# Stick-breaking's queries and keys of a head pair in one 512-column product, with four PSUM banks for dense products and two for DeltaNet

## The chip, the cores and the metric

The kernel runs on one core of one Trainium2 chip. Its time is device microseconds (us) of one execution, and the median of several executions is what counts. The engines are TensorE (PE in the profile, with its weight loads as a row of their own, PEld), VectorE (DVE), ScalarE (ACT), GpSimd (POOL) and SyncE (SP), which issues most of the DMAs. PSUM, the memory that matmuls write, has eight banks, each 512 float32 columns wide over 128 partitions.

## What is computed

A decoder trunk of two layers on 512 tokens of width 1024. A layer is a SwiGLU FFN (half step), a mixer with two branches, and a second FFN.

```
def hybrid_mixer(h, w_in, ...):
    dn_qkv, dn_z, dn_b, dn_a, sb_q, sb_k, sb_v, gate_a, gate_b = split_cols(h @ w_in)
    ...                                             # conv + SiLU, L2 norm, decay
    o_a = gated_delta_rule_chunked(q, k, v, g, beta)            # branch A, 8 heads of 128
    y_a = (rmsnorm(o_a, dn_out_norm) * silu(dn_z)) @ w_branch_a
    qb = rmsnorm(to_heads(sb_q, 8, 128), sb_q_norm)             # branch B, 8 heads of 128
    kb = rmsnorm(to_heads(sb_k, 8, 128), sb_k_norm)
    o_b = stick_breaking_attention(qb, kb, to_heads(sb_v, 8, 128))
    y_b = o_b @ w_branch_b
    return (sigmoid(gate_a) * y_a + sigmoid(gate_b) * y_b) @ w_out

x = x + 0.5 * swiglu(rmsnorm(x), ffn1_w_in, ffn1_w_out)
x = x + hybrid_mixer(rmsnorm(x), ...)
x = x + 0.5 * swiglu(rmsnorm(x), ffn2_w_in, ffn2_w_out)
```

## The kernel before

**Dense products.** Every float32 operand is split into a high and a low part (`wh`, `wl` of a weight, `xh`, `xl` of the activation), and a product is three matmuls: high x high, low x high, high x low. ScalarE writes `wh`, VectorE `wl`, from a raw chunk of 1024 elements a partition (512 KB) that SP loads (`fetch`, L635). Two raw chunks and three converted ones are in flight. A "unit" of the mixer is one step of the string `ORDER` (L32), 70 letters that set the order of dense work within a mixer: D, G, Z and B units give 128 output columns over all tokens, feature-major (weights stationary, 512 tokens moving, 8 x 3 = 24 matmuls of 512 columns, one PSUM bank). D is a third of a DeltaNet head (q, k or v), G a branch gate, Z the DeltaNet output gate, B a piece of branch B's projection.

**Stick-breaking's units** (S, L1435) are token-major: tokens are stationary and 256 weight columns (two heads) move. Three S units in turn give a head pair's q, k and v. A unit has 2 chunks x 4 token blocks x 4 k-tiles x 3 = 96 matmuls of 256 columns, and fills two banks, each with two token blocks side by side (`proj_tm`, L772). Of q and k ScalarE evacuates a bank with four squares that sum as they go (`sbsq`, for the norms) and then one copy (`sraw`). After k the chain of that pair starts (`sb_chain`, `sb_head`).

**Work between dense matmuls.** The program is laid out ahead of time: `Weave` holds a model of every engine's time, and after each dense matmul (each third one in `proj_tm`) `tick` lets pending chains issue the steps that the model says are ready. TensorE's instructions run in that fixed order. Chains are the evacuations (`evac`, in order), weight conversions (`ahead`), the stick-breaking chain, and the DeltaNet chain of a head pair (`dn_chain`, L1167): norms (`pk`, `kw`), decays (`pd`), scores (`pq`, `lt`), an inverse by 31 steps on VectorE (`it`, `itmp`), two levels of blocks (`pp`, `pt_`), the recurrence over four token blocks (`pa`, then `rhs` and `qs`, then `py`, `po_`; `dn_recur`, L1355) and the output (`oT`, `oa`). A pair's scores wait until the pair before has done its levels (`dn_at`). `until` lets chains go on without dense work: a D unit that begins a pair waits so for the pair two before it, the letter C for the stick-breaking chains, and E drains everything left.

**PSUM.** Three pools (L362 to L364): `acc` with 3 banks for dense products, `dps` with 3 for DeltaNet, `sps` with 2 for the stick-breaking chain. `dps` also serves the FFN's second sum (`ps`), the transposes of x at the start (`xps`), and small sums. A chain asks for a tile with `room`, which waits in the model until the oldest tile of a full pool was last used; `bank` (L731) does the same for dense products by a count of evacuations that are pending.

Of the kernel before, what the change touches and what calls it, by code (L numbers as in the profile page):

```python
# [8 lines left out]
F32 = mybir.dt.float32  # L9
# [6 lines left out]
P = 128  # L16
# [12 lines left out]

ORDER = "DSDDDDGDSDSDDDDDSGSGSZSDSZSDDDSDGDSDDDGDDZDGZSGGZGZCGGGBBBBBBBBEZGGZGG"  # L32
SQ = 4
CB = 3


# [306 lines left out]
class Trunk:  # L343
    def __init__(self, ctx, tc, depth, w):
        self.tc = tc
        self.nc = self.weave = Weave(tc.nc)
        self.w = {n: [m[l] for l in range(depth)] for n, m in w.items()}
        self.ctx = ctx
        e = ctx.enter_context
        self.cst = e(self.pool("cst", 1))  # L350
        self.xop = e(self.pool("xop", 1))
        self.wp = e(self.pool("wp", 3))
        dram = e(tc.tile_pool(name="scr", bufs=1, space=bass.MemoryType.DRAM))
        self.scr_in = dram.tile([32, 32, 32], F32, name="scr_in")
        self.scr_out = dram.tile([32, 32, 32], F32, name="scr_out")
        self.osp = dram.tile([2, KD, P, SEQ], F32, name="osp")
        self.ysp = dram.tile([KD, P, SEQ], F32, name="ysp")
        self.gsp = dram.tile([NG, P, SEQ], F32, name="gsp")
        self.zsp = dram.tile([HEADS, P, SEQ], F32, name="zsp")
        self.xsp = dram.tile([KD, P, SEQ], F32, name="xsp")  # L360
        self.stat = e(self.pool("stat", 1))
        self.acc = e(self.pool("acc", 3, space=PSUM))  # L362
        self.dps = e(self.pool("dps", 3, space=PSUM))
        self.sps = e(self.pool("sps", 2, space=PSUM))  # L364
        self.order = list(self.weight_order(depth))
        self.chunks = iter([c for c in self.order if len(c) == 5])
        self.turn = iter(self.order)
        self.raws = []
        self.parts = []
        self.rings = ([], [])  # L370
        self.hid = None
        self.r = None
        self.evacs = [0, 0]
        self.convs = self.conv_done = 0
# [224 lines left out]
    def weight_order(self, depth):  # L599

        w = self.w

        def ffn(w_in, w_out):
            for kind, a, *b in PLAN:
                if kind == "c":
                    yield w_in, 0, KD, a % 2 * DFF + a // 2 * P, P
                elif kind == "s":
                    yield a, b[0]
                elif b[1] == 0:
                    yield (w_out,) + SECTIONS[a] + (b[0] * P, P)  # L610

        for l in range(depth):
            yield from ffn(w["ffn1_in"][l], w["ffn1_out"][l])
            yield w["in"][l], 0, KD, 4 * D, 16
            count = dict.fromkeys(ORDER, 0)
            for kind in ORDER:
                n = count[kind]
                count[kind] += 1
                if kind == "D":
                    yield w["in"][l], 0, KD, (1, 0, 2)[n % 3] * D + n // 3 * P, P  # L620
                elif kind == "S":
                    for k0 in (0, 4):
                        yield w["in"][l], k0, 4, N_SB + n % 3 * D + n // 3 * 2 * P, 2 * P
                elif kind == "G":
                    yield w["in"][l], 0, KD, N_GA + n * P, P
                elif kind == "Z":
                    yield w["in"][l], 0, KD, 3 * D + n * P, P
                elif kind == "B":
                    yield w["b"][l], 0, KD, n * P, P
            for m in ("a", "out"):  # L630
                for n in range(KD):
                    yield w[m][l], 0, KD, n * P, P
            yield from ffn(w["ffn2_in"][l], w["ffn2_out"][l])

    def fetch(self):  # L635
        c = next(self.chunks, None)
        if c is None:
            return
        src, k0, nk, c0, n = c
        raw = self.wp.tile([P, nk, n], F32, tag="raw", bufs=2, name="raw")  # L640
        self.nc.sync.dma_start(
            raw, src[k0 * P:(k0 + nk) * P, c0:c0 + n].rearrange("(k p) n -> p k n", p=P))
        self.raws.append(raw)

    def ahead(self):
# [84 lines left out]

    def bank(self, shape, n=1):  # L731

        self.weave.until(lambda: self.evacs[0] - self.evacs[1] <= 3 - n)
        return self.acc.tile(shape, F32, tag="acc", name="pf")

    def evac(self, engine, f):
# [35 lines left out]
    def proj_tm(self, ready=lambda: True):  # L772
# [20 lines left out]
            used[0] = True  # L793
        self.weave.until(ready)
        return out


    def fetch_fours(self):
# [633 lines left out]

    SBG = (((3, 0, 512),), ((2, 0, 384),), ((1, 0, 256), (0, 256, 128)))

    def sb_unit(self, l, n):  # L1435

        nc = self.nc
        m = self.sb
        pr, w = n // 3, n % 3
        if w == 0:  # L1440
            self.weave.until(lambda: self.weave.done(("sb", pr % 2)))
            self.sbq = dict(ss=m.tile([P, NTB, 4], F32, tag="sbss", bufs=2, name="sbss"))
        st = self.sbq
        if w < 2:
            pts = self.proj_tm()
            raw = st[w] = m.tile([P, NTB, 256], F32, tag=f"raw{w}", bufs=2, name="sraw")
            def half(a):
                sq = self.stat.tile([P, 2, 2, P], F32, tag="junk", name="sbsq")
                for b in range(2):
                    for hh in range(2):  # L1450
                        nc.scalar.activation(sq[:, b, hh, :], pts[a][:, b, hh * P:(hh + 1) * P], AF.Square,
                                             accum_out=st["ss"][:, 2 * a + b, 2 * w + hh:2 * w + hh + 1])
                nc.scalar.copy(raw[:, 2 * a:2 * a + 2, :], pts[a])

            self.evac("scalar", lambda: half(0))
            self.evac("scalar", lambda: half(1))
            if w == 1:
                chain = self.weave.after(("sb", pr % 2), self.sb_chain(l, pr, st))
                self.weave.spawn(self.weave.after("sb", self.weave.then("evac", chain)))
            return  # L1460
        pts = self.proj_tm(lambda: self.weave.done(("sb", (pr + 1) % 2)))
        vh = m.tile([P, NTB, 256], F32R, tag="vh", bufs=1, name="vh")
        vl = m.tile([P, NTB, 256], F32R, tag="vl", bufs=1, name="vl")
# [10 lines left out]
        self.evac("scalar", lambda: half(0))  # L1474
        self.evac("scalar", lambda: half(1))

    def sb_chain(self, l, pr, st):
        nc = self.nc
        m = self.sb
# [9 lines left out]
        for hh in range(2):  # L1489
            for w in range(2):  # L1490
                for b in range(NTB):
                    v = st[w][:, b, hh * P:(hh + 1) * P]
                    s = y[:, b, 2 * w + hh:2 * w + hh + 1]
                    nc.scalar.activation(v, v, AF.Copy, scale=s)
                yield 0
            yield from self.sb_head(l, pr * 2 + hh, hh, st)

    def sb_head(self, l, h, hh, st):
# [4 lines left out]
        for w in range(2):  # L1503
            yield from self.sps.room("sp")
            ps = self.sps.tile([P, SEQ], F32, tag="sp", name="qk_ps")
            for b in range(NTB):
                nc.tensor.transpose(ps[:, b * P:(b + 1) * P], st[w][:, b, cs], self.ident)
            hi = m.tile([P, SEQ], F32R, tag=f"qkh{w}", bufs=1, name="qkh")
            lo = m.tile([P, SEQ], F32R, tag=f"qkl{w}", bufs=1, name="qkl")
            g = (self.sbg if w == 0 else self.vcol["sbk"])[:, l:l + 1]  # L1510
# [159 lines left out]
    def mixer(self, l, gain_next):  # L1670
# [4 lines left out]
        with self.pool("mx", 1, reuse_waits="tile") as self.mx:  # L1675
# [12 lines left out]
            for kind in ORDER:  # L1688
# [3 lines left out]
                if kind == "D":  # L1692
                    self.dn_unit(l, n, first[1] if n == 0 else None)
                elif kind == "S":
                    self.sb_unit(l, n)
                elif kind in "GZ":
                    self.gate(kind, n)
                elif kind == "C":
# [138 lines left out]
```

## Time and profile before

| what | value |
|---|---|
| median of 3 runs (lowest to highest) | 2801.56 us (2798.18 to 2802.18) |
| the profiled execution: its time, its span | 2801.22 us, 2799.4 us |
| TensorE busy, instructions | 2755.9 us (98%), 17249 |
| weight loads, DVE, ACT, POOL busy | 2449.7, 2009.1, 1468.2, 232.9 us |
| mixer of layer 0 | about 378 to 1055 us from the span's start |
| mixer of layer 1 | about 1763 to 2440 us |
| DMA | 312.46 MB, 112 GB/s |

How to read a row: a group of instructions shows its engine, operation, what it writes and reads (`pf<-xh,wh`: into the dense tile pf, moving xh, stationary or second operand wh), the shape, the count, busy time and mean duration, and the idle time of the engine before it with what ended it. All kernel lines appear as L286, the helper that issues them, so groups are told apart by the names of their tiles. Busy times of matmuls overlap, since a matmul's end is modelled.

### The profile page before, as it was taken

The numbers are of one execution on the slowest core, as the hardware profiler recorded it, in microseconds if no ns is written. First come the engines' busy times: TensorE is split into PE (matmuls) and PEld (weight loads), VectorE is DVE, ScalarE is ACT, GpSimd is POOL, SyncE is SP. The second block draws the span as 40 slices with busy tenths as digits, with TensorE's granted clock in tenths as the row PEclk, the third lists the DMA queues.
The fourth block names the chain that finished last, engine by engine and source line by source line (L and its number), as shares of the span: only waits on it lengthen the run. The fifth ranks groups of instructions, "written<-read, shape, count | busy, mean of one in ns | idle before, by whom it ended". The sixth has DMA issues, their size and how long they took to land.

```text
span 2799.4 us, 44209 instructions
## 1 busy us (share of the span) xinstructions
PE 2755.9 (98%) x17249; PEld 2449.7 (88%) x17249; DVE 2009.1 (72%) x3154; ACT 1468.2 (52%) x2953; POOL 232.9 (8%) x243
## 2 busy tenths in 40 slices
PE   8999999999999999999999999999999999999999
PEld 7999988888888887999979999889988888879998
DVE  6877576886777557867678676778878765588664
ACT  4444346767664644544445344468675745445333
POOL 4000020000100031000010000110001001210000
PEclk9999999999999999999999999999999999999999
DMA  4333143323335654333143331423323358433332
GB/s 145 117 106 111 39 121 92 91 80 88 89 101 180 225 170 128 102 106 106 49 136 102 105 107 54 114 80 86 102 80 94 103 162 285 148 91 112 99 91 64
DMA packets 438017, 312.46 MB, mean 112 GB/s; under 512 B 31706, under 2 KB 408080, under 8 KB 437808
## 3 DMA queue, kind: packets, MB, share of 16 engines
q1 hardware_dynamic: 436432, 308.99, 37.1%
q8 instruction: 135, 2.21, 0.3%
q10 hardware_dynamic: 1088, 0.53, 0.1%
q14 instruction: 74, 0.61, 0.1%
q0 software_dynamic: 288, 0.12, 0.0%
HBM read 276.03 MB, written 33.55 MB: 111 GB/s over the span
## 4 chain that ended last, share of the span: by engine, by line
PE 86%; DVE 9%; ACT 3%; DMA 1%; issue 1%; ACTq 0%; DVEq 0%
PE pf L286 56%; PE pq L286 16%; PE ps L286 7%; DVE wl L286 1%; DVE itmp L286 1%; ACT u L286 1%; PE sbo_ps L286 1%; DVE sbs L286 1%; DVE qkv L286 1%; PE z_ps L286 1%; DVE it L286 1%; DMA raw<-in_ffn_w_out_dram 1%; PE pa L286 1%; PE at_ps L286 0%; DVE tl L286 0%
## 5 line engine op out<-in xcount | busy, mean ns | idle before, releaser
L286 ACT ACTIVATE wh<-raw 128x1024 fp32r<-128x1024 f32 (+2 forms) x352 | 337.1, 959 | 314.9 <-PE pf L286 147.4
L286 PE MATMUL pf<-xh,wh 128*128 128x512 f32 (+1 forms) x1312 | 487.8, 372 | 0.4 <-DVE t L286 0.4
L286 DVE TENSOR_TENSOR wl<-raw,wh 128x1024 fp32r<-128x1024 f32 (+2 forms) x351 | 402.4, 1147 | 117.7 <-ACT wh L286 115.0
L286 PE MATMUL pf<-xh,wl 128*128 128x512 f32 (+1 forms) x1312 | 485.5, 370 | 1.3 <-DVE wl L286 1.3
L286 PE MATMUL pf<-xl,wh 128*128 128x512 f32 (+1 forms) x1312 | 484.4, 369 | 0.0
L286 PE MATMUL pf<-hp,wh 128*128 128x512 f32 x1408 | 440.9, 394 | 4.6 <-ACT wh L286 4.6
L286 PEld LDWEIGHTS pf<-hp,wh 128*128 128x128 f32 x1408 | 265.8, 190 | 61.1 <-ACT wh L286 6.3
L286 DVE TENSOR_TENSOR wl<-sraw,wh 128x1024 fp32r<-128x1024 f32 x216 | 263.5, 1221 | 52.3 <-ACT wh L286 52.3
L286 ACT ACTIVATE wh<-sraw 128x1024 fp32r<-128x1024 f32 x216 | 228.2, 1056 | 137.8 <-PE pf L286 104.9
L286 PE MATMUL pf<-hp,wl 128*128 128x512 f32 x704 | 277.0, 393 | 9.1 <-DVE wl L286 9.1
L286 PEld LDWEIGHTS pf<-xh,wl 128*128 128x128 f32 x1312 | 247.7, 189 | 41.4 <-DVE wl L286 2.8
L286 PEld LDWEIGHTS pf<-xh,wh 128*128 128x128 f32 x1312 | 247.9, 189 | 39.5 <-issue 2.2
L286 PEld LDWEIGHTS pf<-xl,wh 128*128 128x128 f32 x1312 | 247.9, 189 | 38.9 <-issue 1.2
L286 PE MATMUL pq<-tl,wh 128*128 128x256 f32 x864 | 244.5, 283 | 0.0
L286 PE MATMUL pq<-th,wl 128*128 128x256 f32 x864 | 244.5, 283 | 0.0
L286 PE MATMUL pq<-th,wh 128*128 128x256 f32 x864 | 244.5, 283 | 0.0
L286 PE MATMUL pf<-wh,xh 128*128 128x256 f32 x768 | 226.7, 295 | 0.0
L286 PE MATMUL pf<-wl,xh 128*128 128x256 f32 x768 | 218.7, 285 | 0.0
L286 PE MATMUL pf<-wh,xl 128*128 128x256 f32 x768 | 218.3, 284 | 0.0
L286 DVE SCALAR_TENSOR_TENSOR x<-pf,x 128x512 f32<-128x512 f32 x128 | 87.8, 688 | 132.8 <-PE pf L286 132.6
L286 PEld LDWEIGHTS pf<-hp,wl 128*128 128x128 f32 x704 | 133.8, 190 | 39.0 <-DVE wl L286 11.0
L286 PEld LDWEIGHTS pq<-th,wh 128*128 128x128 f32 x864 | 165.9, 192 | 0.2
(1098 smaller groups left out, 6079.6 us busy)
## 6 DMA issues: line engine op xcount, KB each, us to landing
sraw<-in_ffn_w_in_dram SPq DMA_DIRECT2D x144, 512.0 KB, 3.6
raw<-in_w_in_dram SPq DMA_DIRECT2D x144, 512.0 KB, 3.9
raw<-in_ffn_w_out_dram SPq DMA_DIRECT2D x96, 384.0 KB, 3.5
raw<-in_ffn_w_in_dram SPq DMA_DIRECT2D x32, 512.0 KB, 4.0
raw<-in_ffn_w_out_dram SPq DMA_DIRECT2D x32, 256.0 KB, 2.9
gsp<-gt SPq DMA_DIRECT2D x32, 256.0 KB, 3.3
of<-osp SPq DMA_DIRECT2D x32, 256.0 KB, 4.2
raw<-in_w_branch_b_dram SPq DMA_DIRECT2D x16, 512.0 KB, 4.1
```

The source lines that it names most:

```text
L286: return f(*args, **kw)
```

## The change

The letter S now means q and k of a pair together, and a new letter V stands for v. In `ORDER` each q unit is taken out, the joint unit is written where k's stood, and v's S becomes V. A joint unit has 4 chunks (two k-tiles each, 256 columns of q and 256 of k side by side) x 4 token blocks x 2 k-tiles x 3 = 96 matmuls of 512 columns, and holds four banks, one a token block, from its first chunk to its last. `acc` gets four banks and `dps` two. ScalarE first copies a bank and then takes the squares from the copy. `proj_tm` and the V unit's body stay as they were.

```diff
@@ -29,8 +29,9 @@
 
 
 
-ORDER = "DSDDDDGDSDSDDDDDSGSGSZSDSZSDDDSDGDSDDDGDDZDGZSGGZGZCGGGBBBBBBBBEZGGZGG"
+ORDER = "DDDDDGDSDVDDDDDGSGVZDSZVDDDDGDSDDDGDDZDGZVGGZGZCGGGBBBBBBBBEZGGZGG"
 SQ = 4
+ACC = 4
 CB = 3
 
 
@@ -359,8 +360,8 @@
         self.zsp = dram.tile([HEADS, P, SEQ], F32, name="zsp")
         self.xsp = dram.tile([KD, P, SEQ], F32, name="xsp")
         self.stat = e(self.pool("stat", 1))
-        self.acc = e(self.pool("acc", 3, space=PSUM))
-        self.dps = e(self.pool("dps", 3, space=PSUM))
+        self.acc = e(self.pool("acc", ACC, space=PSUM))
+        self.dps = e(self.pool("dps", 2, space=PSUM))
         self.sps = e(self.pool("sps", 2, space=PSUM))
         self.order = list(self.weight_order(depth))
         self.chunks = iter([c for c in self.order if len(c) == 5])
@@ -619,8 +620,13 @@
                 if kind == "D":
                     yield w["in"][l], 0, KD, (1, 0, 2)[n % 3] * D + n // 3 * P, P
                 elif kind == "S":
+
+                    both = w["in"][l][:, N_SB:N_SB + 2 * D].rearrange("k (w c) -> k w c", w=2)
+                    for k0 in range(0, KD, 2):
+                        yield both[:, :, n * 2 * P:(n + 1) * 2 * P], k0, 2, None, 4 * P
+                elif kind == "V":
                     for k0 in (0, 4):
-                        yield w["in"][l], k0, 4, N_SB + n % 3 * D + n // 3 * 2 * P, 2 * P
+                        yield w["in"][l], k0, 4, N_SB + 2 * D + n * 2 * P, 2 * P
                 elif kind == "G":
                     yield w["in"][l], 0, KD, N_GA + n * P, P
                 elif kind == "Z":
@@ -638,8 +644,13 @@
             return
         src, k0, nk, c0, n = c
         raw = self.wp.tile([P, nk, n], F32, tag="raw", bufs=2, name="raw")
-        self.nc.sync.dma_start(
-            raw, src[k0 * P:(k0 + nk) * P, c0:c0 + n].rearrange("(k p) n -> p k n", p=P))
+        rows = src[k0 * P:(k0 + nk) * P]
+        if c0 is None:
+            for w in range(2):
+                self.nc.sync.dma_start(raw[:, :, w * n // 2:(w + 1) * n // 2],
+                                       rows[:, w].rearrange("(k p) c -> p k c", p=P))
+        else:
+            self.nc.sync.dma_start(raw, rows[:, c0:c0 + n].rearrange("(k p) n -> p k n", p=P))
         self.raws.append(raw)
 
     def ahead(self):
@@ -730,7 +741,7 @@
 
     def bank(self, shape, n=1):
 
-        self.weave.until(lambda: self.evacs[0] - self.evacs[1] <= 3 - n)
+        self.weave.until(lambda: self.evacs[0] - self.evacs[1] <= ACC - n)
         return self.acc.tile(shape, F32, tag="acc", name="pf")
 
     def evac(self, engine, f):
@@ -793,6 +804,30 @@
             used[0] = True
         self.weave.until(ready)
         return out
+
+    def proj_qk(self, out):
+
+        nc = self.nc
+        pss = []
+        for k0 in range(0, KD, 2):
+            wh, wl, used = self.next_weights()
+            for b in range(NTB):
+                ts = slice(b * P, (b + 1) * P)
+                if k0 == 0:
+                    pss.append(self.bank([P, SEQ], b + 1))
+                for k in range(2):
+                    xh, xl = self.xh[k0 + k][:, ts], self.xl[k0 + k][:, ts]
+                    nc.tensor.matmul(pss[b], xh, wh[:, k, :], start=k0 + k == 0, stop=False)
+                    self.weave.tick()
+                    nc.tensor.matmul(pss[b], xl, wh[:, k, :], start=False, stop=False)
+                    self.weave.tick()
+                    nc.tensor.matmul(pss[b], xh, wl[:, k, :], start=False, stop=k0 + k == KD - 1)
+                    self.weave.tick()
+                if b == 0:
+                    self.ahead()
+                if k0 + 2 == KD:
+                    out(b, pss[b])
+            used[0] = True
 
 
     def fetch_fours(self):
@@ -1432,32 +1467,11 @@
 
     SBG = (((3, 0, 512),), ((2, 0, 384),), ((1, 0, 256), (0, 256, 128)))
 
-    def sb_unit(self, l, n):
+    def sb_unit_v(self, l, n):
 
         nc = self.nc
         m = self.sb
-        pr, w = n // 3, n % 3
-        if w == 0:
-            self.weave.until(lambda: self.weave.done(("sb", pr % 2)))
-            self.sbq = dict(ss=m.tile([P, NTB, 4], F32, tag="sbss", bufs=2, name="sbss"))
-        st = self.sbq
-        if w < 2:
-            pts = self.proj_tm()
-            raw = st[w] = m.tile([P, NTB, 256], F32, tag=f"raw{w}", bufs=2, name="sraw")
-            def half(a):
-                sq = self.stat.tile([P, 2, 2, P], F32, tag="junk", name="sbsq")
-                for b in range(2):
-                    for hh in range(2):
-                        nc.scalar.activation(sq[:, b, hh, :], pts[a][:, b, hh * P:(hh + 1) * P], AF.Square,
-                                             accum_out=st["ss"][:, 2 * a + b, 2 * w + hh:2 * w + hh + 1])
-                nc.scalar.copy(raw[:, 2 * a:2 * a + 2, :], pts[a])
-
-            self.evac("scalar", lambda: half(0))
-            self.evac("scalar", lambda: half(1))
-            if w == 1:
-                chain = self.weave.after(("sb", pr % 2), self.sb_chain(l, pr, st))
-                self.weave.spawn(self.weave.after("sb", self.weave.then("evac", chain)))
-            return
+        pr, st = n, self.sbq
         pts = self.proj_tm(lambda: self.weave.done(("sb", (pr + 1) % 2)))
         vh = m.tile([P, NTB, 256], F32R, tag="vh", bufs=1, name="vh")
         vl = m.tile([P, NTB, 256], F32R, tag="vl", bufs=1, name="vl")
@@ -1474,6 +1488,29 @@
         self.evac("scalar", lambda: half(0))
         self.evac("scalar", lambda: half(1))
 
+    def sb_unit_qk(self, l, pr):
+
+        nc = self.nc
+        m = self.sb
+        self.weave.until(lambda: self.weave.done(("sb", pr % 2)))
+        st = self.sbq = dict(ss=m.tile([P, NTB, 4], F32, tag="sbss", bufs=2, name="sbss"))
+        raw = m.tile([P, NTB, SEQ], F32, tag="raw", bufs=2, name="sraw")
+        st["raw"] = raw.rearrange("p b (w c) -> p w b c", w=2)
+
+        def out(b, ps):
+            def f():
+                nc.scalar.copy(raw[:, b, :], ps)
+                sq = self.stat.tile([P, 4, P], F32, tag="junk", name="sbsq")
+                for i in range(4):
+                    nc.scalar.activation(sq[:, i, :], raw[:, b, i * P:(i + 1) * P], AF.Square,
+                                         accum_out=st["ss"][:, b, i:i + 1])
+
+            self.evac("scalar", f)
+
+        self.proj_qk(out)
+        chain = self.weave.after(("sb", pr % 2), self.sb_chain(l, pr, st))
+        self.weave.spawn(self.weave.after("sb", self.weave.then("evac", chain)))
+
     def sb_chain(self, l, pr, st):
         nc = self.nc
         m = self.sb
@@ -1489,7 +1526,7 @@
         for hh in range(2):
             for w in range(2):
                 for b in range(NTB):
-                    v = st[w][:, b, hh * P:(hh + 1) * P]
+                    v = st["raw"][:, w, b, hh * P:(hh + 1) * P]
                     s = y[:, b, 2 * w + hh:2 * w + hh + 1]
                     nc.scalar.activation(v, v, AF.Copy, scale=s)
                 yield 0
@@ -1504,7 +1541,7 @@
             yield from self.sps.room("sp")
             ps = self.sps.tile([P, SEQ], F32, tag="sp", name="qk_ps")
             for b in range(NTB):
-                nc.tensor.transpose(ps[:, b * P:(b + 1) * P], st[w][:, b, cs], self.ident)
+                nc.tensor.transpose(ps[:, b * P:(b + 1) * P], st["raw"][:, w, b, cs], self.ident)
             hi = m.tile([P, SEQ], F32R, tag=f"qkh{w}", bufs=1, name="qkh")
             lo = m.tile([P, SEQ], F32R, tag=f"qkl{w}", bufs=1, name="qkl")
             g = (self.sbg if w == 0 else self.vcol["sbk"])[:, l:l + 1]
@@ -1692,7 +1729,9 @@
                 if kind == "D":
                     self.dn_unit(l, n, first[1] if n == 0 else None)
                 elif kind == "S":
-                    self.sb_unit(l, n)
+                    self.sb_unit_qk(l, n)
+                elif kind == "V":
+                    self.sb_unit_v(l, n)
                 elif kind in "GZ":
                     self.gate(kind, n)
                 elif kind == "C":
```

## The prediction

> **What bounds the kernel now.** I read the page first (busy time, then the chain that ended last), then the two mixers by stretch, then TensorE's own waits.
>
> ```profile
> span 2799.4 us, 44209 instructions
> PE 2755.9 (98%) x17249; PEld 2449.7 (88%) x17249; DVE 2009.1 (72%) x3154; ACT 1468.2 (52%) x2953; POOL 232.9 (8%) x243
> PE 86%; DVE 9%; ACT 3%; DMA 1%; issue 1%; ACTq 0%; DVEq 0%
> 378.00:1055.00 677.00, 669.61 (x4098) 581.46 (x4097) 489.75 (x1003) 415.77 (x1060) 75.12 (x84) 1.00 0.41 121
> 1763.00:2440.00 677.00, 669.11 (x4095) 581.04 (x4094) 489.42 (x1003) 415.58 (x1059) 75.41 (x84) 1.00 0.41 121
> ```
>
> The last two rows are the two mixers (length, then busy PE, PEld, DVE, ACT, POOL, granted clock, DMA): 677 us each, with TensorE idle for 7.4 and 7.9 us of it. So TensorE's stream is the bound, and what an instruction of it costs is the distance from its start to the next start, not its duration (which overlaps).
>
> ```profile
> 386.61 0.28 PE L286 MATMUL pf<-wh,xl 128*128 128x256 f32 x1
> ...
> 393.93 0.28 PE L286 MATMUL pf<-wl,xh 128*128 128x256 f32 x1
> ...
> 395.20 0.40 PE L286 MATMUL pf<-xh,wh 128*128 128x512 f32 x1
> ...
> 412.89 0.39 PE L286 MATMUL pf<-xh,wh 128*128 128x512 f32 x1
> ```
>
> The first pair are matmuls 0 and 61 of an unbroken token-major run: 7.32 us / 61 = 120.0 ns for 256 columns. The second pair are 0 and 78 of a 512-column run: 17.69 / 78 = 226.8 ns. Two halves cost 240.0, one whole 226.8: a fixed 13.2 ns goes with every matmul.
>
> **The change part by part.**
>
> *One product for q and k.* The 256-column token-major matmuls are these three groups:
>
> ```profile
> L286 PE MATMUL pf<-wh,xh 128*128 128x256 f32 x768 | 226.7, 295 | 0.0
> L286 PE MATMUL pf<-wl,xh 128*128 128x256 f32 x768 | 218.7, 285 | 0.0
> L286 PE MATMUL pf<-wh,xl 128*128 128x256 f32 x768 | 218.3, 284 | 0.0
> ```
>
> 2304 in all; two thirds (q, k) = 1536 become 768 of 512 columns, and v's 768 stay. Saved: 768 x 13.2 ns = **-10.1 us**, all on TensorE's stream. The 768 weight loads that go with them lie beside matmuls (PEld is a row of its own and the stream is paced by starts), so nothing more is booked for them. The Trainium skill, page "TensorE: Matmul & The Clock Gate", section "Wait — 56ns, not 53.3ns?", gives the warm spacing as N / 2.4 GHz plus about 2.5 ns. By it one pair would save 2.5 ns and the change 1.9 us, and the time would be 8 us above my sum. The trace disagrees in the constant (13.2 ns), so the sum goes by the rows.
>
> *The order.* Each q unit is dropped and the joint unit stands where k stood; nothing else moves. D17, last of DeltaNet's third pair, thereby comes one 96-matmul unit (96 x 120 ns = 11.5 us) earlier in the dense work; the last pair's D23 keeps exactly the same units behind it. Price 0.
>
> *Evacuation on ScalarE.* Same count of squares and copies, but four banks in a row.
>
> ```profile
> L286 ACT ACTIVATE sbsq<-pf 128x128 f32<-128x128 f32 x128 | 34.3, 305 | 0.2
> L286 ACT ACTIVATION_READ_ACCUMULATOR sbsq<-pf 128x1 f32 x128 | 29.2, 237 | 0.0
> L286 ACT COPY sraw<-pf 128x512 f32<-128x512 f32 x32 | 20.3, 634 | 0.0
> ```
>
> A bank costs 0.63 + 4 x (34.3 + 29.2) / 128 = 2.6 us, four 10.5 us, against banks completed 6 x 0.227 = 1.36 us apart: ScalarE ends some 6 us after the unit. But the copy now comes first and alone reads the bank, so a bank is back 0.63 us after its turn begins. The next unit needs one bank (the first, long free) and the one after, 5.4 us later, the second. Cover: 677 - 415.8 = 261 us of idle ScalarE per mixer. I take 0. Queued behind the burst is the next conversion of weights (wh), on which DVE's wl and then a product wait; the row of that wait below (10.4 us in the whole run) doubling for these 8 of 152 units would be 0.5 us. Opening four banks asks that the unit before is evacuated within 3 x 1.36 = 4.1 us of the start; before, two of three banks were asked at once. Price 0.
>
> *DMA.* 32 chunks of 512 KB become two of 256 KB: 32 more issues on SP's queue.
>
> ```profile
> raw<-in_w_in_dram SPq DMA_DIRECT2D x144, 512.0 KB, 3.9
> L286 SPq DMA_DIRECT2D raw<-in_w_in_dram x146: 367/368/714, 357.7 to 2328.1; - x146
> ```
>
> 32 x 0.37 = 12 us of SP over two mixers; behind them on that queue are the stores of gates and heads and the next chunk. A chunk is consumed in 24 x 0.227 = 5.4 us, lands in 3.9, and two are in flight; 0.37 later is hidden: 0. Without the cover it would be 12 us at most.
>
> *Two banks for everything of the DeltaNet pool.* Four uses.
>
> In the prologue x is transposed through that pool, one bank in turn:
>
> ```profile
> 24.16 0.68 DVE L286 COPY x<-xps 128x512 f32<-128x512 f32 x1
> 24.24 0.40 PE L286 MATMUL adt_ps<-adt_row,ones 1*128 1x32 f32 x2
> ```
>
> With two banks adt_ps takes the one that this last copy of x leaves, at 24.84: 0.6 us late, with the first projection queued behind it: **+0.6**. The FFN's sums hold two banks at a time, and the third asks for the first's some 11 us after its last matmul (four units of 24 x 120 ns): 0.
>
> DeltaNet itself allocates 22 tiles a head, 352 in all. TensorE's own waits now:
>
> ```profile
> PE pf L286 <- DVE wl L286: 10.4, 6, 2.3
> PE z_ps L286 <- DVE qkl L286: 4.2, 2, 2.4
> PE pk L286 <- ACT qkv L286: 3.1, 4, 1.2
> PE at_ps L286 <- DVE al L286: 2.3, 2, 1.2
> PE py L286 <- DVE rhs L286: 2.2, 2, 1.1
> PE pq L286 <- ACT qkv L286: 0.7, 2, 0.3
> PE pa L286 <- DVE s L286: 0.2, 1, 0.2
> ```
>
> DeltaNet (pk, py, pq, pa) waits 6.2 us / 352 = 18 ns a tile with three banks; the stick-breaking chain, in a pool of two, 6.5 us (z_ps, at_ps) / 144 tiles = 45 ns. Upper end: 352 x 27 ns = +9.7. Lower end: the waits that there are could fall otherwise, -6.2; nothing excludes that, since a new order re-deals them. Which is nearer? In the recurrence the two heads run in step and a third tile is wanted when the first has been read:
>
> ```profile
> L286 DVE SCALAR_TENSOR_TENSOR rhs<-pa,neg,qkv x48: 341/351/353, 566.0 to 2308.3; 128x128 f32<-128x128 f32 x48
> L286 ACT ACTIVATE qs<-pa,eg x48: 350/367/370, 566.4 to 2308.7; 128x128 f32<-128x128 f32 x48
> ```
>
> py needs rhs anyway, and with two banks qs as well: 0.4 us more of the chain's latency a step, during which TensorE goes on with dense matmuls. So it is latency more than idle time, nearer the low end: **+3**. The fourth dense bank buys nothing visible: where a dense product waits, the rows above name its weights (wl), not a bank.
>
> *Sum.* 2801.2 (this execution: span 2799.4 and 1.8 around it; the median of the runs shown is 2801.56) - 10.1 + 0.6 + 3 = **2794.7**.
>
> **The rivals.**
>
> *Two-bank waits take all of it.* The upper end above: 2801.2 - 10.1 + 0.6 + 9.7 = 2801.4. For it: a wait has a second price here.
>
> ```profile
> 502.14 0.50 PE L286 MATMUL z_ps<-qkl,qkh 128*128 128x512 f32 x1 [1.80 <-DVE qkl L286]
> 500.00:520.00 20.00, 18.20 (x119) 16.99 (x119) 19.55 (x36) 12.74 (x34) 0.00 (x0) 0.91 0.20 54
> ```
>
> After that 1.80 us wait the granted clock is 0.91 over 20 us, 1.8 us lost. The same page of the Trainium skill, section "A second HAM failure mode: psum-queue depth-cycling", speaks against this change: short idle times between groups that cycle through PSUM banks re-throttle the clock. One such drop per mixer is all the trace has so far. Against: the latency argument.
>
> *DeltaNet's tail outlasts its cover (slower).* At the end of the ORDER's first part the program drains DeltaNet without dense work.
>
> ```profile
> L286 ACT COPY kw<-pk x8: 606/646/688, 440.2 to 795.1; 128x512 f32<-128x512 f32 x8
> L286 DVE SCALAR_TENSOR_TENSOR lt<-pq,e x16: 412/418/425, 451.6 to 828.6; 128x256 f32<-128x256 f32 x16
> 930.44 0.61 PE L286 MATMUL oT<-ident,qkv 128*128 128x128 f32 x4
> 932.76 0.39 PE L286 MATMUL pf<-sph__9428,wl 128*128 128x512 f32 x1
> 932.99 0.39 PE L286 MATMUL pf<-xh,wh 128*128 128x512 f32 x1
> ```
>
> The last head's transposes (oT) stand only 932.99 - 930.44 = 2.5 us ahead of the drain. A last pair that is d later idles TensorE d - 2.5 us a layer, plus 1.8 for the clock. With d = 9 (22 tiles of 0.4 us) that is 2 x (6.5 + 1.8) = 16.6: 2811. It decides from d = 6.8 on (2 x 6.1 makes up the 6.5 saved and 5.6 more). Against: the last pair's scores come 33 us after its norms (795.1 to 828.6), because they wait for the third pair, which now starts 11.5 us sooner.
>
> *A 512-column token-major matmul saves nothing* (240 ns, the mechanism by which the skill's constant would nearly hold): 2801.2 + 3.6 = 2804.8. Against: both rows above are of the same engine, weights and precision.
>
> *The new order drops the waits.* If the 1.80 us wait and its clock drop vanish in both mixers: 2794.7 - 7.2 = 2787.5.
>
> **How the numbers follow.** A measurement of this kernel can tell about 0.2%, 5.6 us, from no change: faster is below 2796.0, slower above 2807.2. Forecast 0.47 (own range 2790 to 2798, so a fifth of it counts as same); two-bank waits 0.25; tail 0.13; no saving 0.05; waits dropped 0.10. Faster 0.38 + 0.10 + 0.02 of the two-bank case = 0.50; same 0.09 + 0.20 + 0.05 = 0.34; slower 0.13 + 0.03 of the two-bank case = 0.16. The range, 2785 to 2806, takes in all but most of the tail case and a little of the others.
>
> **What the changed profile would show.** Right: 768 matmuls of 128x512 with the stationary xh or xl, 226 to 228 ns apart; 768 fewer PE instructions; the two mixers about 5 us shorter each minus waits; FFN stretches as before; adt_ps some 0.6 us late. Two-bank waits: pk, pq, pa, py rows with more than 10 us among TensorE's waits, or more stretches below clock 0.95. Tail: oT within or after the last product of branch b, with TensorE idle before the next gate. Wrong altogether if the dense products wait for a bank (a pf row waiting for ACT sraw), or if wh conversions behind ScalarE's burst hold a product.

## The result and the profile after

| | before | after |
|---|---|---|
| median of the runs (lowest to highest) | 2801.32 us (2798.18 to 2802.18) | 2901.80 us (2898.17 to 2906.94) |
| profiled span, mean granted clock | 2799.4 us, 0.995 | 2899.3 us, 0.981 |
| TensorE busy, instructions | 2755.9 us, 17249 | 2800.0 us, 16481 |

The changed kernel takes 1.0361 times as long (95% interval 1.0345 to 1.0376): 100 us more, where 6.5 us less was forecast.

The page of the changed kernel, its head and the shares of the chain that ended last:

```profile
span 2899.3 us, 42615 instructions
PE 2800.0 (97%) x16481; PEld 2435.1 (84%) x16481; DVE 2012.0 (69%) x3154; ACT 1479.7 (51%) x2953; POOL 232.8 (8%) x243
PE 75%; DVE 15%; ACT 6%; issue 2%; DMA 1%; POOL 0%; ACTq 0%; SPq 0%; DVEq 0%; POOLq 0%
```

768 matmuls fewer; VectorE and ScalarE run as many instructions as before and are busy for nearly as long (2009.1 and 1468.2 us then). But in the chain DVE stands at 15% where it had 9%, and ACT at 6% for 3%: TensorE now waits for them. Two sums can be read from the page alone. TensorE's idle time, span less busy, went from 43.5 to 99.3 us (+55.8). The time that the clock took, span x (1 - clock), went from 14.0 to 55.1 us (+41). Together these are 97 of the 99.9 us by which the span grew. This is an estimate: half speed is counted also where TensorE sat idle (4.0 us of the stretch from 591.91 to 598.74 below stand in both sums), and the product's saving and waits too short to leave idle time in the record stand in neither.

Where: each mixer ends where the sum for the next norm (`ssps`) starts on TensorE. Timeline of the kernel before, then of the changed one, first mixer, then the second one of the changed kernel:

```profile
377.43 0.68 PE L286 MATMUL ssps<-ssq,ones 128*128 128x512 f32 x1
1055.80 0.70 PE L286 MATMUL ssps<-ssq,ones 128*128 128x512 f32 x1 [0.21 <-DVE ssq L286]
```
```profile
379.75 0.68 PE L287 MATMUL ssps<-ssq,ones 128*128 128x512 f32 x1
1106.59 0.67 PE L287 MATMUL ssps<-ssq,ones 128*128 128x512 f32 x1 [0.30 <-DVE ssq L287]
...
1811.87 0.67 PE L287 MATMUL ssps<-ssq,ones 128*128 128x512 f32 x1
...
2540.03 0.67 PE L287 MATMUL ssps<-ssq,ones 128*128 128x512 f32 x1 [0.30 <-DVE ssq L287]
```

The first mixer went from 678.4 to 726.8 us, and the second is 728.2. All else together grew by some 2 us.

What TensorE waited for in the changed kernel (us in total, times, longest):

```profile
PE pf L287 <- DVE wl L287: 10.9, 6, 3.4
PE po__5658 L287 <- ACT y L287: 6.8, 1, 6.8
PE po__19263 L287 <- ACT y L287: 6.8, 1, 6.8
PE pk L287 <- ACT qkv L287: 6.6, 3, 3.2
PE pq L287 <- ACT qs L287: 6.5, 4, 2.3
PE oT L287 <- ACT qkv L287: 5.9, 2, 3.0
...
PE pt__6606 L287 <- ACT p L287: 2.7, 1, 2.7
...
PE py L287 <- ACT qs L287: 2.4, 10, 0.3
...
PE adt_ps L287 <- PE vp L287: 0.6, 1, 0.6
...
PE pf L287 <- ACT sraw L287: 0.5, 1, 0.5
```

The weights' row (wl) is what it was (10.4). New are DeltaNet's: its output sum po for y, its scores pq for `qs` (the old reader of the bank that pq takes), its transposes oT. The dense products hardly wait for a bank (sraw 0.5).

The worst place is the first pair's recurrence. Timeline of TensorE there, then of ScalarE, then of VectorE (start, length, instruction, and in brackets the idle time ahead of it and its releaser):

```profile
584.47 3.23 PE L287 MATMUL pq<-qkv 128*128 128x256 f32 x8 [2.34 <-ACT qs L287]
595.90 0.80 PE L287 MATMUL po__5658<-yw,kw 128*128 128x128 f32 x2 [6.81 <-ACT y L287]
```
```profile
584.57 0.47 ACT L287 ACTIVATE vh<-pf,rc 128x256 fp32r<-128x256 f32 x1
593.54 0.84 ACT L287 ACTIVATE vh<-pf,rc 128x256 fp32r<-128x256 f32 x2 [8.50 <-DVE vl L287]
...
595.59 0.27 ACT L287 COPY y<-py 128x128 f32<-128x128 f32 x1
```
```profile
586.03 0.42 DVE L287 SCALAR_TENSOR_TENSOR lt<-pq,e 128x256 f32<-128x256 f32 x1 [3.44 <-PE pq L287]
...
588.40 0.68 DVE L287 SCALAR_TENSOR_TENSOR u<-z_ps,u 128x512 f32<-128x512 f32 x1
...
593.04 0.47 DVE L287 SCALAR_TENSOR_TENSOR vl<-pf,rc,vh 128x256 fp32r<-128x256 f32 x1
```

Read them as one loop. TensorE's pq waits 2.34 us for a DeltaNet bank. VectorE sits idle 3.44 us for that pq (lt), with six steps of the stick-breaking chain and a vl queued behind the scores. ScalarE, in a V unit's evacuation, doesn't write the next vh until VectorE has done that vl: 8.50 us, with DeltaNet's y behind it in its queue. And TensorE's next step is the po that needs y: 6.81 us, with no dense product ahead of it. Three queues, each in order, hang on one another. The late bank is 2.34 us of this by these rows; from 586.03 to 593.51 us VectorE does what stands in its own queue, but for 0.95 us.

The clock follows. Stretches of the changed kernel (length, busy PE, PEld, DVE, ACT, POOL, granted clock, DMA):

```profile
554.36:557.77 3.41, 2.32 (x43) 2.10 (x43) 2.69 (x7) 2.76 (x12) 0.00 (x0) 1.00 0.84 226
557.77:568.01 10.24, 10.24 (x59) 8.78 (x59) 4.73 (x24) 5.08 (x17) 1.94 (x2) 0.50 0.14 43
568.01:585.08 17.07, 13.56 (x95) 12.14 (x94) 7.46 (x18) 9.19 (x24) 0.14 (x1) 1.00 0.11 31
585.08:588.49 3.41, 3.41 (x10) 2.55 (x8) 1.51 (x5) 0.00 (x0) 0.63 (x1) 0.50 0.00 0
588.49:591.91 3.42, 0.52 (x3) 0.30 (x2) 3.32 (x5) 0.00 (x0) 0.64 (x1) 1.00 0.02 5
591.91:598.74 6.83, 2.83 (x11) 2.64 (x12) 3.77 (x10) 4.25 (x12) 0.00 (x0) 0.50 0.00 0
```

The record gives the clock in steps of 3.41 us: it is 1.00 or 0.50, and in these rows each half-speed stretch follows on one in which TensorE ran thin (2.32 of 3.41 us busy, then 10.24 us at half).

### The profile page after: what moved, and what is told of

The parts are those of the page before. It is cut to its first block, busy times and chain, and to the rows that moved or that the text cites. A ratio compares the mean times of both kernels' runs of the same rounds, so it can differ in the third digit from the quotient of the medians.

```text
span 2899.3 us, 42615 instructions
## 1 busy us (share of the span) xinstructions
PE 2800.0 (97%) x16481; PEld 2435.1 (84%) x16481; DVE 2012.0 (69%) x3154; ACT 1479.7 (51%) x2953; POOL 232.8 (8%) x243
## 4 chain that ended last, share of the span: by engine, by line
PE 75%; DVE 15%; ACT 6%; issue 2%; DMA 1%; POOL 0%; ACTq 0%; SPq 0%; DVEq 0%; POOLq 0%
PE pf L287 46%; PE pq L287 15%; PE ps L287 7%; DVE wl L287 3%; DVE qkv L287 3%; DVE sbs L287 1%; DVE itmp L287 1%; PE sbo_ps L287 1%; DVE dsc L287 1%; ACT wh L287 1%; DVE it L287 1%; DMA raw<-in_ffn_w_out_dram 1%; ACT qkv L287 1%; ACT sbsq L287 1%; PE z_ps L287 1%
## 5 line engine op out<-in xcount | busy, mean ns | idle before, releaser
L287 PEld LDWEIGHTS pf<-xl,wh 128*128 128x128 f32 x1312 | 249.1, 190 | 39.4 <-issue 1.0
L287 PE MATMUL pf<-wh,xh 128*128 128x256 f32 (+1 forms) x512 | 180.5, 353 | 0.0
L287 PE MATMUL pf<-wh,xl 128*128 128x256 f32 (+1 forms) x512 | 177.1, 346 | 0.0
L287 PE MATMUL pf<-wl,xh 128*128 128x256 f32 (+1 forms) x512 | 177.1, 346 | 0.0
L287 PEld LDWEIGHTS pq<-th,wl 128*128 128x128 f32 x864 | 165.9, 192 | 0.5 <-DVE wl L287 0.5
```

Of the source, the lines that this page charges most:

```text
L287: return f(*args, **kw)
```

## The experiments

In the first four runs theory A is that the lost DeltaNet bank makes the waits, B that it is something of the joint product, and C that it is the order of the units; the later runs name theirs anew. Times are medians; the kernel before stood at 2800.0 to 2801.1 us beside every one of them.

**Two banks alone, and order alone.** The kernel before with one half of the change each. In the second, q and k stay two products of 256 columns, and q stands just ahead of k.

```
e1:  self.dps = e(self.pool("dps", 3 -> 2, space=PSUM))
e2:  ORDER = "DDDDDGDSSDSDDDDDGSSGSZDSSZSDDDDGDSSDDDGDDZDGZSGGZGZCGGGBBBBBBBBEZGGZGG"
```

> The kernel before with one edit: two PSUM banks in DeltaNet's pool in place of three (one bank unused; separate q and k units, old order, three dense banks). Theory A, the bank: where two head pairs overlap, four heads share two banks, TensorE stops in program order at tiles whose bank is still being read, and the pair's chain comes late; then this alone costs what the change lost plus the 10 us that the joint product saves: 2895 to 2920 us. Theory B, the joint product (four banks held, ScalarE's burst of 10.5 us): this stays within 2801 to 2815. Theory C, the order: 2801 to 2810.

Measured: 2871.1 us, ratio 1.0253 (1.0238 to 1.0268): +71 us.

> The kernel before with the new order alone: each q unit (256 columns) moved to just ahead of its k unit, three DeltaNet banks, three dense banks. A and B: 2795 to 2808, a re-dealing of waits. C, the order (DeltaNet's third pair 11.5 us sooner, q and k evacuated in a row): most of the loss, 2850 to 2900.

Measured: 2852.2 us, ratio 1.0186 (1.0171 to 1.0201): +52 us. TensorE's waits, of the first and then of the second:

```profile
PE py L286 <- ACT qs L286: 8.5, 14, 2.8
PE pq L286 <- ACT y L286: 5.9, 2, 2.9
...
PE pq L286 <- DVE qkv L286: 4.3, 2, 2.2
```
```profile
PE oT L286 <- ACT qkv L286: 7.5, 2, 3.7
PE pk L286 <- ACT qkv L286: 7.2, 3, 3.4
PE z_ps L286 <- DVE sbs L286: 6.1, 6, 2.3
```

With two banks the tile that comes next (py, pq) waits for the reader of the tile before. With the new order there are three banks, and TensorE waits for inputs instead (oT, pk for qkv). In the new order D1 to D5, D12, D16 and D17 all come a q unit sooner, not D17 alone. Either half alone costs half of the loss or more, with different waits. The first time lies in none of the ranges, and the second in C's, which expected next to nothing of the first: no single theory was right. 71 + 52 - 10 = 113, against the 100 measured. What the joint product costs for itself was not measured apart: no run has it with the old order and DeltaNet's three banks at all times.

**The bank looked for again.** `room` asks the plan once when the oldest tile of a full pool is free, and waits that long. Here it asks again until one is free.

```
-        if len(ring) == (bufs or self.bufs):
+        while len(ring) == (bufs or self.bufs):
...
-            if t > w.t:
+            if t <= w.t:
+                break
```

> The changed kernel with one edit: a chain that waited for room in a pool looks again when it goes on, and waits on if another chain has taken the freed bank in the meantime (before: one look, then the tile is taken and TensorE waits for it in program order). A1, the loss is TensorE standing still behind such tiles: most of it comes back, 2795 to 2825. A2, the loss is the longer chains themselves (two banks cannot feed four heads, wherever the wait stands): 2850 to 2895. B: 2890 to 2905, unchanged.

> Control: the kernel before, three DeltaNet banks, with the same second look for room. All theories: 2795 to 2808; if the second look helps by itself with three banks, below 2795.

Measured: 2879.5 us, ratio 1.0283 (1.0268 to 1.0299), so 22 us come back in the changed kernel; and 2800.9 us, 1.0003 (0.9993 to 1.0012), in the kernel before. The first lies in A2's range. With three banks the first answer does; with two, some of the loss is a plan that asks for a bank that is not free. Most of it remains.

**Bank and order, two by two.** f1, g3 and f2 below have the joint product with DeltaNet on three banks that it takes in turn. Dense products have three, where the changed kernel has four. The joint product borrows one of DeltaNet's for its first token block and gives it back after that block's copy. f3 is the changed kernel with the new ORDER alone.

```
-ACC = 4
+ACC = 3
-        self.dps = e(self.pool("dps", 2, space=PSUM))
+        self.dps = e(Turns(self.weave, self.tc.tile_pool(name="dps", bufs=1, space=PSUM), 3))
-                    pss.append(self.bank([P, SEQ], b + 1))
+                    pss.append(self.bank([P, SEQ], b) if b else self.borrow())
f3, g3: ORDER = "DDDDDDGSDDDDDDVGSGVGGSDDDGVDDDDDDDDSDZZGVZGGGZZCGZGBBBBBBBBEZGGZGG"
```

> The changed kernel with its own ORDER, but DeltaNet keeps three banks that it takes in turn, dense products have three, and the joint product borrows one DeltaNet bank for its first token block, from its first matmul to that block's copy. So the product (-10) and the order (+52 measured alone) are there and the permanent loss of a bank is not. Theory A (two separate causes, order and banks, that add up): 2801 - 10 + 52 = 2843, between 2830 and 2858. Rival B (the banks are the one cause with the joint product, whose four-bank burst is costly for itself): 2870 to 2905, since the joint product still takes a bank from DeltaNet for some 25 us at a time.

> The changed kernel with two DeltaNet banks, and an ORDER of the same letters dealt again for two banks. Theory A (the banks are a cause of their own, 71 us when taken alone): the order's part comes back and most of the banks' part stays, 2835 to 2872. Rival (two banks only cost because the order was dealt for three): 2790 to 2815.

> The ORDER of the run with two banks and a redealt order (2833.7), but with three DeltaNet banks of which the joint product borrows one, as in the two runs before that. It takes the permanent loss of the bank away and leaves the order. Theory A (the bank is worth about what it cost alone, also in this order): 2788 to 2805. Rival B (the dealing of the units against the chains' work is all that counts, and this one was dealt for two banks; lending a bank disturbs as much as lacking it): 2822 to 2860.

| joint product, with | order of the change | order dealt again | the order is worth |
|---|---|---|---|
| two DeltaNet banks | 2901.8 | 2833.7 | 68 |
| a third one, lent at times | 2858.0 | 2807.9 | 50 |
| the bank is worth | 44 | 26 | |

Ratios to before: f1 1.0198 (1.0181 to 1.0216), f3 1.0121 (1.0104 to 1.0137), g3 1.0025 (1.0014 to 1.0035). Each theory that named one cause fell: f3 ended between its two ranges and g3 between its own, and f1 at the very edge of A's. Bank and order are both causes, and they are not independent: the worth of either depends on the other. In the table "the bank" is the whole edit, with dense products on three banks of their own instead of four.

**A better plan is not a better kernel.**

> As the run before it, with another ORDER: the same letters, dealt again so that the kernel's own plan gives a mixer no longer than it gave the kernel before. Theory A (order and banks are all of the loss): the product's 10 us are seen at last, 2801 - 10 + 0.6 = 2791, between 2786 and 2798. Rival B (the joint product costs for itself, in its evacuation or in the banks that it holds): 2805 to 2870. Rival C (the plan's length does not tell what the chip does, so that any new order costs some tens of us): 2815 to 2860.

Measured: 2850.4 us, ratio 1.0177 (1.0159 to 1.0196): in the ranges of rival B and of rival C. g3, with the same joint product and lent bank, took 2807.9, so 42 us of this go with the order. This ORDER ("DDDDSDGDDVDDDDDGSGVGGSDVDDDDDDSGDDGDDGDGVZGGZZZCGZZBBBBBBBBEZGGZGG") was dealt so that the program's own plan was as short as that of the kernel before. Its ScalarE groups show one thing that the plan hadn't:

```profile
L287 ACT ACT_TABLE_LOAD x37 | 47.5, 1283 | 5.7 <-DVE v_n L287 5.0
L278 ACT ACT_TABLE_LOAD x14 | 18.0, 1283 | 0.3
```
```profile
439.20 0.63 ACT L287 ACTIVATE u<-u 128x512 f32<-128x512 f32 x1
439.85 1.28 ACT L287 ACT_TABLE_LOAD   x1
441.14 0.63 ACT L287 ACTIVATE u<-u 128x512 f32<-128x512 f32 x1
```

51 loads of function tables at 1.28 us, where every other kernel here has 35 (21 and 14): 16 more, 20.5 us of ScalarE. The timeline of ScalarE shows where: eight a mixer, from 425.50 to 453.41 us in the first, stand between steps of the stick-breaking chain (`sby`, `u`, `sbs`), which by the kernel's code takes exp and ln in turn. In this ORDER the first pair's chain runs ahead of the table load that the program itself issues (L278, at 459.50 us); in the changed kernel that load comes first (426.8 us), and the chain's steps follow without one. How much of the loss that makes wasn't tried apart.

**One unit moved.** The kernel before with the third pair's q unit behind the D unit that begins the third DeltaNet pair (`...SZSDSZS...` to `...SZDSSZS...`).

> The kernel before with one unit moved: the third pair's q unit now stands behind the DeltaNet unit that begins the third DeltaNet pair (and that waits for the first pair to be done), so that this unit and its wait come 11.5 us sooner in the dense work. Theory O1 (the order's loss sits at that wait): 25 us or more of the 52 us. Theory O2 (the loss is spread over all four moved units): about 13 us, 2808 to 2818. Theory O3 (it comes from the first two pairs' units, which shift DeltaNet's first pair): under 6 us.

Measured: 2809.2 us, 1.0029 (1.0018 to 1.0039): 8.6 us. That is within O2's range, at its lower end, and far from O1: the order's loss doesn't sit at that one wait. The other three units weren't moved alone.

**The loop through three queues.** First vh and vl as a tile for each token block, so that vh has no tile to wait for.

```
-        vh = m.tile([P, NTB, 256], F32R, tag="vh", bufs=1, name="vh")
+        vh = [m.tile([P, 256], F32R, tag=f"vh{b}", bufs=1, name="vh") for b in range(NTB)]
```

> The kernel before with one edit: vh and vl of a V unit are a tile for each token block in place of one tile for all four, so that ScalarE's next vh no longer waits for VectorE's vl of the block before. It is the control for the next run. Theory A (that wait only costs where a chain on TensorE's path stands behind it on ScalarE; the trace of before has no such place): 2796 to 2803. Rival (the wait costs everywhere): below 2795.

> The changed kernel with the same edit. In its first mixer ScalarE stands 8.5 us at a vh behind VectorE's vl, with the first DeltaNet pair's y queued behind it, and TensorE then stands 6.8 us at po. Theory A (three queues in order hold one another up, and this is the link): 6.8 us and some clock come back in each mixer, 2875 to 2890. Rival B (VectorE's own length of work holds the first pair, ScalarE only waits elsewhere): 2895 to 2907.

> The changed kernel with two DeltaNet banks and the redealt ORDER (2833.7) with the same edit. Theory A: little of that kernel's idle time stands at this link, 2824 to 2834. Rival B: below 2820, if the link is what is left.

Measured: 2800.7 us, 0.9998 (0.9989 to 1.0008); 2901.5 us, 1.0354 (1.0332 to 1.0376); 2832.1 us, 1.0112 (1.0095 to 1.0129). Nothing moved, and this is no verdict for B: the wait itself stayed, as the timeline of ScalarE in g1 shows.

```profile
589.22 0.84 ACT L287 ACTIVATE vh<-pf,rc 128x256 fp32r<-128x256 f32 x2 [7.27 <-DVE vl L287]
```

So the tile vh was not what it waited for. vh and vl of a block also read the same dense bank, in turn. The row fits that: of its two vh the second, which reads the other bank, doesn't wait for the vl of the first. Why two reads of one bank come in turn is not shown. The next edit, on top of this one, writes both vh of a bank ahead of both vl.

```
             for b in (2 * a, 2 * a + 1):
                 nc.scalar.activation(vh[b], src, AF.Copy, scale=rc)
+            for b in (2 * a, 2 * a + 1):
                 nc.vector.scalar_tensor_tensor(vl[b], pts[a][:, b % 2, :], ...)
```

> The changed kernel; in a V unit both vh of a bank come ahead of both vl, so that ScalarE doesn't stand at a vh behind VectorE (7.3 to 8.5 us at the first pair's recurrence, with y behind it). Theory A (this link of queues carries TensorE's 6.8 us wait at po and what follows): that wait goes in both mixers, 2 x (6.8 + some 3 of clock) = 20 us less, 2875 to 2888. Rival B (the first pair is late for VectorE's work and for the bank that pq waits for; taken away here, the wait turns up at the next step): 2893 to 2906.

> The kernel before with both vh ahead of both vl. Theory A (the wait only costs where a DeltaNet step on TensorE's path stands behind it, which the trace of before doesn't show): 2796 to 2803. Rival B (the edit is worth as much anywhere): 2770 to 2785.

Measured: the changed kernel 2874.3 us, 1.0261 (1.0247 to 1.0275), 27.5 us less, just beyond theory A's range; the kernel before 2791.9 us, 0.9967 (0.9954 to 0.9979), 9 us less, between its two ranges. The timelines of TensorE and of ScalarE at the same place in the changed kernel with the edit, and then the 20 us around it as a stretch:

```profile
581.72 3.50 PE L287 MATMUL pq<-qkv 128*128 128x256 f32 x8 [2.34 <-ACT qs L287]
```
```profile
581.82 1.57 ACT L287 ACTIVATE vh<-pf,rc 128x256 fp32r<-128x256 f32 x4
585.71 0.37 ACT L287 ACTIVATE yw<-py,dsc 128x128 f32<-128x128 f32 x1 [2.32 <-PE py L287]
585.97 0.26 ACT L287 COPY y<-py 128x128 f32<-128x128 f32 x1
```
```profile
580.00:600.00 20.00, 15.48 (x76) 12.01 (x76) 14.47 (x33) 13.66 (x45) 2.39 (x7) 0.91 0.23 59
```

All four vh run together, y starts 4.25 us after pq where it started 11.12 us after it, po no longer waits, and these 20 us hold 76 matmuls at a clock of 0.91. In the changed kernel, where this place comes 2.75 us later, they held 47 at 0.74:

```profile
580.00:600.00 20.00, 10.77 (x47) 9.02 (x46) 10.23 (x24) 8.58 (x22) 1.27 (x2) 0.74 0.14 33
```

The loop is shown: breaking one link of it returned 27.5 us, of which the changed kernel's own share, less what the kernel before gains too, is 18. The pq that waits 2.34 us for a bank is still there, so po's 6.81 us came of the link, not of that wait alone. The control came out against its expectation, though the trace of before does name the link, among ScalarE's waits:

```profile
ACT vh L286 <- DVE vl L286: 25.9, 16, 6.4
```

With the edit that row is gone, and so are two of TensorE's in the kernel before, py for rhs (2.2 us) and at_ps for al (2.3 us). What such a wait on ScalarE costs can't be read from its length: 34.9 us of it in the changed kernel were worth 27.5, 25.9 before were worth 9, and 39.4 in h2 below were worth 4.

**Can the product's 10 us be had?** Lent bank, the units dealt a second time, for a plan that stays short when VectorE and ScalarE are slower than planned; then with the vh edit; then with one gate unit moved from ahead of the second joint unit to behind it.

```
h2, h3: ORDER = "DDDDDDGSDDDDDDVGSVGGSDGDGDDDVDDDDDDSDGGZVGZGZZZCGGZBBBBBBBBEZGGZGG"
h4:     ORDER = "DDDDDDGSDDDDDDVSGVGGSDGDGDDDVDDDDDDSDGGZVGZGZZZCGGZBBBBBBBBEZGGZGG"
```

> Three DeltaNet banks of which the joint product borrows one, as in the run of 2807.9, with the units dealt once more, for a plan that stays short when VectorE and ScalarE are slower than planned. Theory A (bank and order are the whole loss, the product saves its 10 us): 2790 to 2800. Rival B (the joint product has a cost of its own, or lending costs): 2803 to 2815. Rival C (a new order always costs on the chip): above 2815.

> The run before it with both vh ahead of both vl. Theory A (the link only costs where a DeltaNet step stands behind it): within 4 us of that run. Rival: 8 us or more below it.

> The kernel of 2800.0 with one gate unit moved from ahead of the second joint unit to behind it. Theory A (the 2.8 us wait of a dense product for the gate's bank in each mixer holds what is missing of the product's gain): 2792 to 2797. Rival B (the wait moves to the next evacuation on VectorE, which is at full work there): 2798 to 2808.

Measured: 2804.1 us, 1.0015 (1.0006 to 1.0024); 2800.0 us, 0.9998 (0.9988 to 1.0007); 2814.7 us, 1.0049 (1.0034 to 1.0064). h2 is in rival B's range (a cost of the joint product itself or of lending), and h3 is 4.1 us below it, at the edge of theory A. So of the 100 us all but the last can be given back, with the joint product in place. But the fair partner of h3 is the kernel before with the same vh edit, 2791.9, and against that it is still 8 us behind. TensorE's waits in h3 name dense products that wait for a bank, which the kernel before doesn't have:

```profile
PE pf L287 <- DVE gt L287: 6.2, 3, 2.8
...
PE pf L287 <- ACT sraw L287: 3.2, 2, 1.6
```

h4 was to take the first away. It put vl in gt's place (pf waiting for DVE vl, 4.7 us in all) and was 15 us slower. The wait moved as rival B has it, but the time is above both ranges, and where the rest comes from stays open. The fastest kernel here is thus the one without the joint product and with the vh edit, 2791.9 us. Whether the 8 us are a cost of the joint product, of lending or of the order, and whether there is an order in which the product's saving is seen, stays open.

## Why the prediction was wrong, step by step

*The product: held as a pace, not seen in a time.* The 512-column token-major matmuls with stationary weights xh and xl follow one another as forecast. The first and last of 11 in a row, in the changed kernel's timeline:

```profile
423.65 0.39 PE L287 MATMUL pf<-wh,xh 128*128 128x512 f32 x1
...
425.92 0.39 PE L287 MATMUL pf<-wh,xl 128*128 128x512 f32 x1
```

2.27 us / 10 = 227 ns (forecast 226 to 228), and there are 768 fewer instructions. By that the -10.1 us of TensorE's stream stands; but no kernel here is 10 us faster for it, so that it reaches the end is not shown.

*Prologue +0.6: held* (the row of adt_ps, 0.6). *ScalarE's evacuation 0 and four dense banks 0: held* for what they named: pf waits 0.5 us for sraw, and 10.9 for wl, where 10.4 was before.

*"Two banks, +3, latency more than idle time": the step that failed first.* Alone it is +71, beyond the upper end of 9.7 as well. The end was made from mean waits, 27 ns more for each of 352 tiles, as if a wait spread evenly. It falls on few tiles (14 waits of py, 4 of pq) and is 2 to 3 us each where it counts. And the sentence that TensorE "goes on with dense matmuls" meanwhile is wrong for this kernel. TensorE's instructions run in the order that the program laid out, so that when qs is late, everything behind py and pq is late, dense products too (2.34 us ahead of pq at 584.47, 2.8 ahead of a py in e1). Idle time (+35.7 us) and clock (+11.8) make 47.5 of the 68.0 us by which e1's profiled span grew; the rest is not put down to any row here.

*"The order, price 0": failed too.* It measured +52 alone. The step counted what stands behind the last pair, overlooked that the first pair's D units move too, and didn't ask what the moved units had covered. By e2's rows they were work that TensorE did while VectorE and ScalarE were busy with a pair's chain (oT, pk, z_ps wait now); that is a reading, since one of the four units alone (8.6 us) is all that was moved apart.

*The clock was seen and mis-sized.* The forecast priced it in rivals alone, at 1.8 us a mixer. It took some 41 us more of the span, nearly as much as the idle time itself.

*The slower rival had the wrong place.* It put the loss at the drain ahead of the gates (2811). The waits stand at the first pair's recurrence and at later pairs' norms, long before the drain; the mark for "two-bank waits", more than 10 us in the rows of pk, py, pq and pa, is met (6.6 + 6.5 + 2.4 in the rows above), but the largest single one, po for y, was in no list.

*The skill's rule.* The Trainium skill, "TensorE: Matmul & The Clock Gate", section "A second HAM failure mode: psum-queue depth-cycling", was weighed against the change and put aside as one drop per mixer. What the traces show is nearer to that section's warning than to the weight that the forecast gave it: short idle times between groups, and a mean clock of 0.981 for 0.995. Fewer banks are not needed for it here: e2, with DeltaNet's three, has a clock of 0.988.

## What to carry to other kernels

In a program laid out by hand or by a plan, a unit that is moved or a buffer that is taken away costs what it had covered, not what it does. Before either, look at the queues that feed TensorE in that stretch, and price a bank at the longest waits that its readers make there, not at the mean over all tiles, with a range for the clock on top (nothing to nine tenths of the added idle time in the table below). No forecast here was made that way, so this is advice and not a tested rule. When a wait is odd (ScalarE for VectorE, with TensorE behind), follow it round the queues: the cheapest fix may be a few lines at one link, as here.

## What the hardware showed that was not expected

The granted clock has two values in these records, 1.00 and 0.50, in stretches of 3.41 us or two or three of them. Some idle times of 2 to 3 us are followed by half speed, and so is a stretch in which TensorE had many small waits (2.32 busy of 3.41 us ahead of a drop of 10.24 us); others are not. The 1.80 us wait of z_ps behind which the kernel before dropped stands in the changed kernel too, and the 20 us around it are at full speed; so are 21 us of e1 in which TensorE was idle for 6.5 and pq waited 2.93 us at a stretch.

```profile
513.33 0.50 PE L287 MATMUL z_ps<-qkl,qkh 128*128 128x512 f32 x1 [1.80 <-DVE qkl L287]
510.00:530.00 20.00, 17.80 (x82) 14.29 (x81) 19.59 (x31) 9.64 (x18) 0.00 (x0) 1.00 0.34 97
```
```profile
569.00:590.00 21.00, 14.46 (x82) 11.63 (x80) 11.55 (x24) 10.70 (x25) 1.27 (x2) 1.00 0.14 32
```

What decides it is not shown. So the price of idle time is not constant. In the whole of the profiled execution, by span less busy and span x (1 - clock):

| kernel | TensorE idle, us | lost to the clock, us |
|---|---|---|
| before | 43.5 | 14.0 |
| g3, lent bank, order dealt again | 51.5 | 11.2 |
| f3, two banks, order dealt again | 56.3 | 25.5 |
| e2, order alone | 68.0 | 34.2 |
| e1, two banks alone | 79.2 | 25.8 |
| h1, changed, vh ahead of vl | 81.7 | 40.2 |
| after | 99.3 | 55.1 |

In g3 8 us of further idle time came with no loss of clock; in the others the clock took between a third and nine tenths of the further idle time again (e1: 11.8 for 35.7; f3: 11.5 for 12.8). These are rough: the clock's figure has three digits, a step of 2.8 us, and it differs between runs of one kernel (0.987 to 0.991 in e1's four, 0.977 to 0.983 in the changed kernel's).
